# Attention with TensorE's order written out: eight transposes, logits of queries to come, value products of one step back

## The chip, the core and the metric

The kernel runs on one core of one Trainium2 chip. The metric is the device time of one execution in microseconds. The median of three runs of the kernel before is 3243.35 us (3238.03 to 3252.03).

## What is computed

One layer of a decoder trunk over 2048 tokens of 1024 channels in float32: a sparse attention mixer, then a SwiGLU feed-forward network, each followed by a LayerNorm. The change lies in the attention. Each query keeps its 256 best admissible keys (an indexer scores them), and 16 heads attend to the kept keys alone:

```python
_, sel = lax.top_k(score, topk)
valid = sel <= qp[None, :, None]
c_sel = jax.vmap(lambda cb, ib: cb[ib])(c_kv, sel)
logits = jnp.einsum('bqhc,bqkc->bhqk', ql, c_sel).astype(jnp.float32)
dist = (qp[None, :, None] - sel).astype(jnp.float32)
logits = logits - slopes[None, :, None, None] * dist[:, None]
logits = jnp.where(valid[:, None], logits, -jnp.inf)
p = jax.nn.softmax(logits, axis=-1).astype(c_sel.dtype)
return jnp.einsum('bhqk,bqkc->bqhc', p, c_sel)
```

## The kernel before, in words

The program has four stages in a row: projections and indexer scores; attention; the output projection; the feed-forward network. Nothing is gathered in attention. For each block of 128 queries a matrix S (SBUF, one row per query, one column per key up to the query's own block) ends up with the negative distance for a kept key and a very large negative number for every other key (the bit search of `topk_bits`, lines 412 to 454, then `select`, lines 490 to 504). All keys are then computed, and the others get probability zero.

`attention` (line 507) is called three times: for queries 0 to 1023, 1024 to 1535 and 1536 to 2047. Its unit is a group: 256 queries (two blocks, i = 0 and 1) for one pair of heads (e = 0 and 1), of which there are eight. The outer loop runs over pairs and, within a pair, over groups; in the second and third call the first group of some or all pairs is done ahead of the second (`EARLY`). A group does this:

- **Logits**, per head and block, and in the second and third call per half of the keys (a piece): GpSimd scales S by the head's slope into a tile `sm` (line 552, 14 buffers); TensorE multiplies queries `aqd` by keys `kka` or `kkb` into the PSUM tile `big` of two banks, two buffers (line 562, 128 output columns of the array); VectorE adds the two and reduces to the row's extreme `mx` (line 563); ScalarE takes the exponential in place with a row sum (line 567).
- **Transposes**: for each block of 128 keys (a key block) four 128x128 transposes of `sm`, two heads by two query blocks, go into one PSUM bank `tp` of three (line 585), and a copy moves it to `pt` (line 587, four buffers; on ScalarE in the first two calls, on ScalarE or VectorE as the scheduler chooses in the third).
- **Value products**: two products per key block, one for each head, accumulate into `oc` (line 589). Each has only 64 output columns (the head's width), head 0 in the lower and head 1 in the upper half of the partitions; each stands in the trace as two instructions. At the group's end VectorE copies `oc` out (line 592).

The source writes a group in one piece: all logits, then key block by key block transposes, copy, products. A list scheduler, which runs when the program is built and has its own model of time, takes the instructions by priority (about the order of the source) as their inputs become ready, and sets each engine's fixed order from that. So on TensorE logits of the next group stand among transposes and products of the current one wherever the scheduler put them. The DMA loads of keys (line 528), values (line 533) and queries (line 545) are issued from SyncE's queue.

The bit search for the last four query blocks and the selection for queries 1024 to 2047 run on ScalarE and VectorE at low priority beside the first call and the start of the second (a branch at line 479 is skipped when the search has settled everything).

Of the kernel before, what the change touches and what calls it, by code (L numbers as in the profile page):

```python
# [11 lines left out]
F32 = mybir.dt.float32  # L12
# [7 lines left out]
AF = mybir.ActivationFunctionType  # L20
# [5 lines left out]
P = 128  # L26
# [20 lines left out]
NSM, NAQ, NPT = 14, 2, 4  # L47
EARLY = 0, 5, 8
# [24 lines left out]
def trunk(tc, x, w_in, w_uk, w_uv, kv_g, w_o, w_gu, w_down, lm_g, lm_b, lf_g, lf_b, out, stop=99):  # L73
# [63 lines left out]
    def f(ap):  # L137
        return ap.bitcast(F32)
# [368 lines left out]
    def attention(ak, ap, apb, bk, qlo, nk, bnd, early, between={}):  # L507


        nw = 2 if nk > bnd else 1  # L510
# [5 lines left out]
        for at_, (j, groups) in enumerate(tasks):  # L516
            if at_ in between:
                between[at_]()
            mark["pair"] = tc.cur_priority
            kk, vv = [], []  # L520
            nkt = qlo + 256 * (groups[-1] + 1)
# [13 lines left out]
            for g in groups:  # L535
                q0 = qlo + g * 256
                b0 = q0 // P
                pr = {}
                total = sums_[:, g * 2:g * 2 + 2, 2 * j:2 * j + 2]
                su = ak.tile([P, 2, 2, 2], F32, name="su", tag="su", bufs=2) if nw == 2 else total.rearrange("p i (e w) -> p i e w", w=1)  # L540
                for e in range(2):
                    slope = float(np.float32(2.0 ** (-8.0 * (2 * j + e + 1) / H)))
                    qd = ak.tile([P, 2, 256], F32R, name="aqd", tag="aqd", bufs=NAQ)
                    for r in range(2):
                        nc.sync.dma_start(out=f(qd)[r * HD:(r + 1) * HD], in_=qs[j, :, e * HD:(e + 1) * HD, q0:q0 + 256].rearrange("c d t -> d c t"))
                    mx = ak.tile([P, 2, nw], F32, name="mx", tag="mx", bufs=4)
                    for i in range(2):
                        L = (b0 + i + 1) * P
                        pr[e, i] = []
                        for wi_, (w0, wn) in enumerate([(0, min(L, bnd)), (bnd, L - bnd)][:nw]):  # L550
                            sm = ap.tile([P, 1024], F32, name="sm", tag="sm", bufs=NSM)
                            nc.gpsimd.tensor_scalar(out=sm[:, :wn], in0=S[b0 + i][:, w0:w0 + wn], scalar1=slope, scalar2=1.0, op0=ALU.mult, op1=ALU.mult)  # L552
                            pr[e, i].append((w0, wn, sm))

# [5 lines left out]
                            for (s0, n) in [(0, first), (first, wn - first)][:1 + (wn > first)]:  # L560
                                for c in range(2):
                                    nc.tensor.matmul(o[:, s0:s0 + n], lhsT=qd[:, c, i * P:(i + 1) * P], rhs=kk[wi_][e][:, s0:s0 + n], start=(c == 0), stop=(c == 1))  # L562
                            nc.vector.tensor_tensor_reduce(out=sm[:, :wn], in0=o, in1=sm[:, :wn], scale=-1.0, scalar=mx[:, i, 0:1] if wi_ else 3.0e38,  # L563
                                                           op0=ALU.add, op1=ALU.min, accum_out=mx[:, i, wi_:wi_ + 1])
                    for i in range(2):
                        for wi_, (w0, wn, sm) in enumerate(pr[e, i]):
                            nc.scalar.activation(sm[:, :wn], sm[:, :wn], AF.Exp, bias=mx[:, i, nw - 1:nw], scale=-1.0, accum_out=su[:, i, e, wi_:wi_ + 1])  # L567
                if nw == 2:
                    nc.vector.tensor_reduce(out=total, in_=su, axis=AX.X, op=ALU.add)

                def prob(e, i, kb):
                    for (w0, wn, sm) in pr[e, i]:
                        if w0 <= kb * P < w0 + wn:
                            return sm[:, kb * P - w0:(kb + 1) * P - w0]
                pcopy = nc.scalar.copy if nk < T else nc.any.tensor_copy
                ob = bk("oc")

                for kb in range(b0 + 2):
                    i0 = 1 if kb == b0 + 1 else 0
                    n = (2 - i0) * P  # L580
                    tp = bk("tp")
                    for e in range(2):
                        for i in range(i0, 2):
                            at = e * n + (i - i0) * P
                            nc.tensor.transpose(tp[:, at:at + P], prob(e, i, kb), ident)  # L585
                    pt = ak.tile([P, 512], F32, name="pt", tag="pt", bufs=NPT)
                    pcopy(pt[:, :2 * n], tp[:, :2 * n])  # L587
                    for e in range(2):
                        nc.tensor.matmul(ob[e * HD:(e + 1) * HD, i0 * P:256], lhsT=vv[kb][:, e * HD:(e + 1) * HD],  # L589
                                         rhs=pt[:, e * n:(e + 1) * n], start=(kb == 0), stop=(kb == b0 + 1))  # L590
                ot = ak.tile([P, 256], F32, name="ot", tag="ot", bufs=2)
                nc.vector.tensor_copy(ot, ob[:, :256])  # L592
                store.dma_start(out=os_[j, :, q0:q0 + 256], in_=ot)
# [574 lines left out]
```

## Time and profile before

| | |
|---|---|
| median of 3 runs | 3243.35 us |
| the profiled execution | 3254.72 us, span 3252.9 us |
| TensorE busy, whole span | 3039.8 us (93%) |
| VectorE / ScalarE / GpSimd busy | 2024.7 / 1650.2 / 1557.6 us |
| attention in the span | from about 715 to about 1702 us |

The span runs from the first to the last instruction; 1.8 us of the execution lie around it. Busy times of the engines overlap one another. Windows are given in microseconds from the span's start. A busy TensorE is one with a matmul in flight, ends being modelled, so "busy throughout" doesn't say that the array works at its peak.

### The profile page before, as it was taken

To read this page: it belongs to the slowest core of one execution; us is meant where nothing else is said; L and a number is where in the kernel's file an instruction comes from. 1 tells how busy PE (TensorE), PEld (TensorE's weight loads), DVE (VectorE), ACT (ScalarE), POOL (GpSimd) and SP (SyncE) were. 2 spreads that over 40 slices of the span, in tenths; PEclk is the share of its full clock that TensorE was granted. 3 is DMA by queue.
4 is the path that set the end of the run, shared out by engine and by line. 5 is a ranking of instruction groups with operands and counts; after the bars stand their busy time and mean duration, and the time that the engine had idled before them with its cause. 6 is when DMAs were issued, how large, how long until landed. Compare 5 with 4: busy or idle time off the path is not lost.

```text
span 3252.9 us, 44786 instructions
## 1 busy us (share of the span) xinstructions
PE 3039.8 (93%) x15067; PEld 2283.1 (70%) x15067; DVE 2024.7 (62%) x3025; ACT 1650.2 (51%) x3169; POOL 1557.6 (48%) x1312
## 2 busy tenths in 40 slices
PE   7988889888888999999999989999989999999996
PEld 6777667665555666566667768888768888878875
DVE  3448798899468644444437675555675555336289
ACT  2536758549987777666662233333333333333333
POOL 3423324452234433433316456666776666645475
PEclk9999999989999999999999989999989999999998
DMA  9776556553344554866528643223233232655353
GB/s 293 241 237 196 185 170 187 181 155 106 104 130 128 161 148 118 195 167 171 150 85 252 209 152 110 100 101 104 98 127 109 101 111 92 216 162 175 110 165 134
DMA packets 460730, 499.00 MB, mean 153 GB/s; under 512 B 51408, under 2 KB 332112, under 8 KB 460496
## 3 DMA queue, kind: packets, MB, share of 16 engines
q1 hardware_dynamic: 369280, 359.09, 38.6%
q10 hardware_dynamic: 91216, 137.01, 11.8%
q8 instruction: 120, 1.97, 0.3%
q14 instruction: 114, 0.93, 0.1%
HBM read 359.01 MB, written 136.97 MB: 152 GB/s over the span
## 4 chain that ended last, share of the span: by engine, by line
PE 57%; DVE 7%; DMA 3%; issue 1%; POOL 0%; ACT 0%; SPq 0%; DVEq 0%; ACTq 0%; POOLq 0%
PE mm L221 8%; PE mm L219 8%; PE mm L220 8%; PE oc L589 7%; PE tp L585 7%; PE big L562 5%; PE mm L953 3%; PE mm L955 3%; PE mm L954 3%; PE mm L736 1%; PE mm L737 1%; PE mm L738 1%; DVE cl L144 1%; DVE hx L771 1%; PE tp L955 1%
## 5 line engine op out<-in xcount | busy, mean ns | idle before, releaser
L552 POOL TENSOR_SCALAR sm<-S 128x768 f32<-128x768 f32 (+7 forms) x384 | 330.8, 869 | 600.9 <-PE tp L585 564.2
L219 PE MATMUL mm<-ch,wh 128*128 128x512 f32 x1232 | 486.9, 396 | 16.1 <-ACT ch L766 14.9
L220 PE MATMUL mm<-cl,wh 128*128 128x512 f32 x1232 | 486.6, 395 | 8.0 <-DVE cl L144 5.9
L221 PE MATMUL mm<-ch,wl 128*128 128x512 f32 x1232 | 488.7, 397 | 0.0
L563 DVE CUSTOM_DVE_ANT_0 sm<-big,sm 128x1024 f32<-128x1024 f32 (+7 forms) x256 | 233.5, 922 | 242.2 <-POOL sm L552 125.0
L587 ACT COPY pt<-tp 128x512 f32<-128x512 f32 (+1 forms) x556 | 298.8, 558 | 151.8 <-PE tp L585 140.1
L567 ACT ACTIVATE sm<-sm,mx 128x768 f32<-128x768 f32 (+7 forms) x384 | 344.8, 901 | 56.6 <-DVE mx L563 55.6
L585 PEld LDWEIGHTS tp<-ident,sm 128*128 128x128 f32 x2176 | 234.8, 142 | 191.4 <-issue 181.1
L585 PE MATMUL tp<-ident,sm 128*128 128x128 f32 x2176 | 362.6, 289 | 2.7 <-ACT sm L567 1.8
L144 POOL TENSOR_TENSOR wl<-s,wh 128x512 fp32r<-128x512 f32 x176 | 239.5, 1366 | 192.4 <-ACT wh L819 192.4
L219 PEld LDWEIGHTS mm<-ch,wh 128*128 128x128 f32 x1232 | 234.4, 191 | 69.8 <-ACT ch L766 18.7
L220 PEld LDWEIGHTS mm<-cl,wh 128*128 128x128 f32 x1232 | 234.1, 190 | 66.5 <-DVE cl L144 10.2
L819 ACT CAST wh<-s 128x512 fp32r<-128x512 f32 x176 | 109.2, 621 | 331.3 <-PE mm L221 93.1
L562 PE MATMUL big<-kka,aqd 128*128 128x512 f32 (+3 forms) x896 | 234.9, 386 | 41.8 <-DVE mx L563 22.6
L221 PEld LDWEIGHTS mm<-ch,wl 128*128 128x128 f32 x1232 | 234.4, 190 | 50.4 <-POOL wl L144 0.2
L589 PE MATMUL oc<-pt,vva 128*64 128x256 f32 (+1 forms) x1536 | 237.3, 402 | 12.9 <-DVE ot L592 7.5
L144 POOL TENSOR_TENSOR wl<-wr,wh 128x512 fp32r<-128x512 f32 x132 | 190.9, 1447 | 94.7 <-ACT wh L819 91.5
L144 POOL TENSOR_TENSOR cl<-hx,ch 128x512 fp32r<-128x512 f32 (+2 forms) x106 | 153.2, 1448 | 153.1 <-ACT ch L948 133.1
L352 DVE SCALAR_TENSOR_TENSOR S<-rl,wi,S 128x768 f32<-128x768 f32 (+5 forms) x161 | 195.1, 1224 | 42.4 <-ACT rl L347 41.6
L562 PEld LDWEIGHTS big<-kka,aqd 128*128 128x128 f32 x896 | 157.5, 199 | 74.6 <-DVE mx L563 37.2
L948 ACT CAST ch<-hx 128x512 fp32r<-128x512 f32 (+2 forms) x158 | 94.7, 609 | 212.1 <-PE tp L954 93.8
L345 PE MATMUL big<-kst,qd 128*128 128x512 f32 (+2 forms) x624 | 163.5, 388 | 34.5 <-ACT rl L347 27.2
(293 smaller groups left out, 6703.5 us busy)
## 6 DMA issues: line engine op xcount, KB each, us to landing
wr<-in_f_w_gu SPq DMA_DIRECT2D x44, 1024.0 KB, 5.2
gs<-cc ACTq DMA_DIRECT2D x154, 256.0 KB, 2.0
hx<-gs SPq DMA_DIRECT2D x144, 256.0 KB, 2.9
aqd<-qs SPq DMA_DIRECT2D x256, 128.0 KB, 3.2
wraw<-in_a_w_in SPq DMA_DIRECT2D x56, 512.0 KB, 4.3
kka<-ks SPq DMA_DIRECT2D x96, 256.0 KB, 4.3
hx<-in_f_w_down SPq DMA_DIRECT2D x66, 256.0 KB, 3.0
qd<-qis SPq DMA_DIRECT2D x112, 128.0 KB, 4.6
```

Source lines behind the costliest of these rows:

```text
L144: (eng or nc.vector).tensor_tensor(out=lo, in0=src, in1=f(hi), op=ALU.subtract)
L219: nc.tensor.matmul(o, lhsT=lh, rhs=rh, start=(i == 0), stop=False)
L220: nc.tensor.matmul(o, lhsT=lh, rhs=rl, start=False, stop=False)
L221: nc.tensor.matmul(o, lhsT=ll, rhs=rh, start=False, stop=(i == n - 1))
L352: nc.vector.scalar_tensor_tensor(sv, rl[:, :wn], wi[:, h:h + 1], sv, op0=ALU.mult, op1=ALU.add)
L552: nc.gpsimd.tensor_scalar(out=sm[:, :wn], in0=S[b0 + i][:, w0:w0 + wn], scalar1=slope, scalar2=1.0, op0=ALU.mult, op1=ALU.mult)
L562: nc.tensor.matmul(o[:, s0:s0 + n], lhsT=qd[:, c, i * P:(i + 1) * P], rhs=kk[wi_][e][:, s0:s0 + n], start=(c == 0), stop=(c == 1))
L563: nc.vector.tensor_tensor_reduce(out=sm[:, :wn], in0=o, in1=sm[:, :wn], scale=-1.0, scalar=mx[:, i, 0:1] if wi_ else 3.0e38, op0=ALU.add, ...
L567: nc.scalar.activation(sm[:, :wn], sm[:, :wn], AF.Exp, bias=mx[:, i, nw - 1:nw], scale=-1.0, accum_out=su[:, i, e, wi_:wi_ + 1])
L585: nc.tensor.transpose(tp[:, at:at + P], prob(e, i, kb), ident)
L587: pcopy(pt[:, :2 * n], tp[:, :2 * n])
L589: nc.tensor.matmul(ob[e * HD:(e + 1) * HD, i0 * P:256], lhsT=vv[kb][:, e * HD:(e + 1) * HD], rhs=pt[:, e * n:(e + 1) * n], start=(kb == 0) ...
```

## The change

The three calls stay, and so do the kinds, numbers and sizes of the instructions. The loop over groups is rewritten. Two consecutive key blocks make a step: eight transposes (six in a group's last step), then up to two logits pieces of a later group (`PIECES`, at most one group ahead in the second and third call and two in the first, `AHEAD`, while fewer than 14 `sm` tiles are in use), then the four value products of the step before. From the first step of a call on, `tc.keep_in_program_order` holds TensorE to the order of the source; the other engines' orders are still the scheduler's.

```diff
+PIECES, AHEAD = {1: 2, 2: 2}, {1: 2, 2: 1}
...
+        def pe(ins):
+            if chained:
+                tc.keep_in_program_order(ins)
...
+            def turned(self, s):
+                out = []
+                for kb in (2 * s, 2 * s + 1):
...
+                            pe(nc.tensor.transpose(tp[:, at:at + P], self.prob(e, i, kb), ident))
...
+            def values(self, turned):
+                for kb, i0, n, pt in turned:
...
+                        pe(nc.tensor.matmul(self.ob[e * HD:(e + 1) * HD, i0 * P:256], lhsT=self.vv[kb][:, e * HD:(e + 1) * HD],
+                                            rhs=pt[:, e * n:(e + 1) * n], start=(kb == 0), stop=(kb == self.b0 + 1)))
...
+        for n, grp in enumerate(todo):
+            while not grp.ready:
+                piece()
+            for s in range(grp.steps):
+                now = grp.turned(s)
+                chained.append(1)
+                for _ in range(PIECES[nw]):
+                    if at_ < min(len(todo), n + 1 + AHEAD[nw]) and live[0] < NSM:
+                        piece()
+                behind()
+                behind = lambda grp=grp, now=now: grp.values(now)
+        behind()
```

How this moves TensorE's instructions, in the third call, inside the second groups of the pairs (16 key blocks each). L585 and L617 are the transposes, L562 and L589-with-`big` the logits, L589-with-`oc` and L628 the value products. Before:

```order
L562 MATMUL big<-kkb,aqd 128x512 x4
L562 MATMUL big<-kka,aqd 128x512 x4
L589 MATMUL oc<-pt,vvb 64x256 x2
L585 MATMUL tp<-ident,sm 128x128 x4
L589 MATMUL oc<-pt,vvb 64x128 x2
L585 MATMUL tp<-ident,sm 128x128 x8
L562 MATMUL big<-kkb,aqd 128x512 x2
L562 MATMUL big<-kkb,aqd 128x384 x2
L562 MATMUL big<-kka,aqd 128x512 x4
L589 MATMUL oc<-pt,vva 64x256 x2
L585 MATMUL tp<-ident,sm 128x128 x4
L589 MATMUL oc<-pt,vva 64x256 x2
```

And now:

```order
L617 MATMUL tp<-ident,sm 128x128 x8
L589 MATMUL big<-kka,aqd 128x512 x4
L589 MATMUL big<-kkb,aqd 128x512 x4
L628 MATMUL oc<-pt,vva 64x256 x4
L617 MATMUL tp<-ident,sm 128x128 x8
L628 MATMUL oc<-pt,vva 64x256 x4
L617 MATMUL tp<-ident,sm 128x128 x8
L628 MATMUL oc<-pt,vvb 64x256 x4
```

Products come in fours where they mostly came in twos. Counted over the three calls, unbroken runs of value products on TensorE were 510 and are 294 (of 1152 products). The last three or four steps of a group have no logits, since those of the next group are done by then.

On VectorE, around the branch at line 479 (480 now) that the selection of queries 1024 to 2047 waits for; "ISA sm" is the addition and reduction of one logits piece. Before:

```order
L592 COPY ot<-oc 128x256
L454 SCALAR_TENSOR_TENSOR hit,thr<-it_73,rank,m_6158 128x8
L473 TENSOR_REDUCE worst<-rank 128x1
L563 ISA sm,mx<-big,sm 128x1024
L563 ISA mx 128x1
```

And now:

```order
L455 SCALAR_TENSOR_TENSOR hit,thr<-it_73,rank,m_6158 128x8
L474 TENSOR_REDUCE worst<-rank 128x1
L590 ISA sm,mx<-big,sm 128x768
L590 ISA mx 128x1
L632 COPY ot<-oc 128x256
```

The rows ahead of the branch hold 113 such reductions before and 94 now, so the selection stands about five groups earlier in the work of attention. In the third call VectorE has 52 of the copies to `pt` now and had 20; ScalarE's share falls by the same 32.

## Rows read from the trace of the kernel before

**Rows 1.** Busy time by stretch: the first stretch holds top-k search and selection, the second neither.
```profile
core 0: us, PE busy (x) PEld busy (x) DVE busy (x) ACT busy (x) POOL busy (x), PEclk, DMA share, GB/s
715.00:1100.00 385.00, 330.85 (x1972) 206.48 (x1971) 290.04 (x527) 328.35 (x694) 143.54 (x169) 0.92 0.44 122
1100.00:1705.00 605.00, 597.05 (x3884) 373.71 (x3884) 265.13 (x529) 416.87 (x824) 202.69 (x226) 1.00 0.57 151
```

**Rows 2.** TensorE's waits, 1100 to 1705 (engine line <- releaser: us in total, times, longest).
```profile
PE oc L589 <- ACT pt L587: 4.2, 2, 2.3
PE big L562 <- DVE mx L563: 1.9, 1, 1.9
PE big L562 <- DMA aqd<-qs: 1.0, 1, 1.0
PE tp L585 <- ACT pt L587: 0.9, 1, 0.9
```

**Rows 3.** TensorE's timeline in the third call (start us, length us, engine line op, count).
```profile
1611.47 1.18 PE L562 MATMUL big<-kkb,aqd 128*128 128x512 f32 x4
...
1613.50 0.65 PE L589 MATMUL oc<-pt,vvb 128*64 128x256 f32 x4
...
1615.04 1.09 PE L585 MATMUL tp<-ident,sm 128*128 128x128 f32 x8
1615.88 1.05 PE L562 MATMUL big<-kkb,aqd 128*128 128x512 f32 x4
...
1618.38 0.66 PE L585 MATMUL tp<-ident,sm 128*128 128x128 f32 x4
1618.96 0.65 PE L589 MATMUL oc<-pt,vva 128*64 128x256 f32 x4
1619.55 0.66 PE L585 MATMUL tp<-ident,sm 128*128 128x128 f32 x4
1620.13 1.08 PE L589 MATMUL oc<-pt,vva 128*64 128x256 f32 x8
1621.15 0.66 PE L585 MATMUL tp<-ident,sm 128*128 128x128 f32 x4
1621.56 1.18 PE L562 MATMUL big<-kkb,aqd 128*128 128x512 f32 x4
...
1636.63 1.18 PE L562 MATMUL big<-kkb,aqd 128*128 128x512 f32 x4
```

**Rows 4.** Waits of weight loads, 715 to 1100.
```profile
PEld tp L585 <- issue: 56.6, 154, 0.8
```

**Rows 5.** TensorE's timeline: first and last runs of value products of each stretch.
```profile
733.85 1.12 PE L589 MATMUL oc<-pt,vva 128*64 128x256 f32 x4
...
1098.72 0.44 PE L589 MATMUL oc<-pt,vvb 128*64 128x128 f32 x4
...
1100.84 0.65 PE L589 MATMUL oc<-pt,vva 128*64 128x256 f32 x4
...
1700.98 1.30 PE L589 MATMUL oc<-pt,vvb 128*64 128x256 f32 x12
```

**Rows 6.** Value products alone, by stretch.
```profile
715.00:1100.00 385.00, 118.39 (x760) 41.77 (x760) 0.92 0.44 122
1100.00:1705.00 605.00, 237.46 (x1544) 80.12 (x1544) 1.00 0.57 151
```

**Rows 7.** TensorE's waits, 715 to 1100.
```profile
PE big L562 <- DVE mx L563: 25.3, 26, 3.2
PE big L562 <- DMA aqd<-qs: 15.7, 9, 4.4
PE oc L589 <- DVE ot L592: 7.5, 5, 4.5
```

**Rows 8.** Costliest groups of the page: scaling, exponential, copy to `pt`.
```profile
L552 POOL TENSOR_SCALAR sm<-S 128x768 f32<-128x768 f32 (+7 forms) x384 | 330.8, 869 | 600.9 <-PE tp L585 564.2
...
L567 ACT ACTIVATE sm<-sm,mx 128x768 f32<-128x768 f32 (+7 forms) x384 | 344.8, 901 | 56.6 <-DVE mx L563 55.6
L587 ACT COPY pt<-tp 128x512 f32<-128x512 f32 (+1 forms) x556 | 298.8, 558 | 151.8 <-PE tp L585 140.1
```

**Rows 9.** Groups by line: the read of the exponential's row sum, whole span.
```profile
L567 ACT ACTIVATION_READ_ACCUMULATOR sm<-sm,mx 128x1 f32 x384 | 74.8, 195 | 0.0
```

**Rows 10.** Groups by line, VectorE, 1100 to 1705.
```profile
L563 DVE CUSTOM_DVE_ANT_0 sm<-big,sm 128x1024 f32<-128x1024 f32 (+1 forms) x110 | 122.3, 1112 | 172.1 <-POOL sm L552 101.1 <-PE big L562 68.5 <-POOL hx L682 1.6
L563 DVE CUSTOM_DVE_ANT_0 sm<-big,sm,mx 128x768 f32<-128x768 f32 (+2 forms) x111 | 110.1, 992 | 106.7 <-PE big L562 85.7 <-POOL sm L552 15.1 <-DVE mx L563 2.1
L563 DVE DVE_READ_ACCUMULATOR2_ANT mx<- 128x1 f32 x221 | 18.4, 83 | 0.0
L587 DVE COPY pt<-tp 128x512 f32<-128x512 f32 x20 | 13.8, 689 | 6.2 <-PE tp L585 5.8
```

**Rows 11.** DMA issues of the page: queries (KB each, us to landing).
```profile
aqd<-qs SPq DMA_DIRECT2D x256, 128.0 KB, 3.2
```

**Rows 12.** VectorE's timeline: a scan of the selection.
```profile
1000.86 3.70 DVE L501 TENSOR_TENSOR_SCAN ft<-one,sr,u 128x1280 f32<-128x1280 f32 x1
```

More of the change, by code (lines that the diff above doesn't have):

```diff
@@ L515, in attention, with task @@
         tasks = [(j, first) for j in range(early)] + [(j, second) for j in range(early)] + [(j, range(ng)) for j in range(early, NPAIR)]
-        for at_, (j, groups) in enumerate(tasks):
-            if at_ in between:
-                between[at_]()
+        work = [(i, j, g, g == groups[0], qlo + 256 * (groups[-1] + 1)) for i, (j, groups) in enumerate(tasks) for g in groups]
+        keys, live, chained = {}, [0], []
+        pcopy = nc.scalar.copy if nk < T else nc.any.tensor_copy
+        def pe(ins):
+            if chained:
+                tc.keep_in_program_order(ins)
+        def task(i, j, nkt):
+            if i in between:
+                between[i]()
             mark["pair"] = tc.cur_priority
             kk, vv = [], []
-            nkt = qlo + 256 * (groups[-1] + 1)
             for i, (k0, k1) in enumerate([(0, min(bnd, nkt)), (bnd, nkt)][:nw]):
@@ L534, in attention, with __init__, logits @@
                 vv += [v[:, k] for k in range((k1 - k0) // P)]
[L535 to L538, printed above, removed]
+            return kk, vv
+        class Group:
+            def __init__(self, i, j, g, new, nkt):
+                self.i, self.j, self.g, self.new, self.nkt = i, j, g, new, nkt
+                self.q0 = qlo + g * 256
+                self.b0 = self.q0 // P
+                self.steps = (self.b0 + 2) // 2
+                self.pr = {}
+                self.gen = self.logits()
+                self.ready = False
+            def logits(self):
+                j, g, b0, pr = self.j, self.g, self.b0, self.pr
+                if self.new:
+                    keys[self.i] = task(self.i, j, self.nkt)
+                kk, self.vv = keys[self.i]
                 total = sums_[:, g * 2:g * 2 + 2, 2 * j:2 * j + 2]
@@ L564, in attention @@
                                                            op0=ALU.add, op1=ALU.min, accum_out=mx[:, i, wi_:wi_ + 1])
[L565 to L579, printed above, removed]
+                            if (i, wi_) == (1, nw - 1):
+                                for i_ in range(2):
+                                    for w_, (_, n, sm) in enumerate(pr[e, i_]):
+                                        nc.scalar.activation(sm[:, :n], sm[:, :n], AF.Exp, bias=mx[:, i_, nw - 1:nw], scale=-1.0, accum_out=su[:, i_, e, w_:w_ + 1])
+                                if nw == 2 and e == 1:
+                                    nc.vector.tensor_reduce(out=total, in_=su, axis=AX.X, op=ALU.add)
```

34 lines of the change are left out of this document (26 added, 8 removed).

## The prediction

> **What bounds the kernel now.** I read the busy times by stretch first, because attention is two regimes [rows 1]. From 1100 to 1705 us TensorE is busy 597 of 605 us at a granted clock of 1.00 (the 2.4 GHz level), ScalarE 417, VectorE 265 and GpSimd 203. Nothing but TensorE can set the pace there, and its list of waits adds up to 8 us [rows 2]. From 715 to 1100 us no engine is full: TensorE is busy 331 of 385 us at 0.92, ScalarE 328, VectorE 290, because the top-k search and the selection share ScalarE and VectorE with attention. So I expect the change to act through TensorE's own time in the second stretch, and weakly in the first.
>
> The second view is TensorE's timeline, for what "busy" hides [rows 3]. The instructions don't cost the same in every neighbourhood. A run of value products with four instructions (one key block) takes 0.59 us from its first start to the next instruction (1618.96 to 1619.55), a run of eight 1.02 us (1620.13 to 1621.15). So the second key block costs 0.43, and each run carries 0.15 to 0.16 us that doesn't depend on its length. The transposes ahead of products carry as much: four transposes before products take 0.58 (1618.38 to 1618.96), while four more transposes before logits cost only 0.84 - 0.41 = 0.43 us (1615.04 to 1615.88 with eight, 1621.15 to 1621.56 with four). That is another 0.15. The trace shows the two together as **0.30 us for every separate run of value products**: about half is paid going in and half coming out, where the matmuls change from 128 output columns to 64 and back (128*128 and 128*64 in the rows). The weight loads show it too: those of transposes sit idle with no releaser, 0.37 us on average, 154 times in the first stretch [rows 4]. Between transposes and logits, both of 128 columns, I see no such cost.
>
> **The change part by part.** *The runs of products.* The timeline has 165 runs between 715 and 1100 and 345 between 1100 and 1705 (the first and last of each in [rows 5]), 510 in all, and the order now has 294. The products there are 760 and 1544 instructions [rows 6]; a step of the new order makes one run of eight, so 760 / 8 = 95 and 1544 / 8 = 193, and with the few runs still broken near the calls' first groups 98 and 196.
>
> Second stretch: 345 - 196 = 149 runs at 0.30 us = **45 us less**, all on the engine that sets the end. One group tests it: the 25.16 us from 1611.47 to 1636.63 hold 15 runs, and the new order gives such a group 8, so 7 x 0.30 = 2.1 us less, 23.1 us.
>
> Here a rule says less. The Trainium skill (TensorEngine Tiling (Array Packing), Key Properties) states that a change of the tiling mode drains TensorE, which agrees in kind with [rows 3]. Its page TensorE: Matmul & The Clock Gate (Part 2) gives a pipeline drain as some 128 cycles; two drains at 2.4 GHz are an estimated 0.11 us, and by that figure the 149 runs would give 16 us instead of 45. The measurement is 0.30, and I go by it.
>
> First stretch: 165 - 98 = 67 runs, 20 us of TensorE's time. How much of it counts, the trace doesn't show, since TensorE idles 54 of 385 us there. At the least it is nothing or a loss (ScalarE is busy 85% of the stretch and none of its work goes away); at the most it is the 20 us and about half of the 48 us of waits in [rows 7], since the selection now stands five groups earlier and products read copies that are a whole step old: 45 us. The rows nearest to it are ScalarE's 328 and TensorE's 331 us, level with each other, so I take a good third of the 20 us, **8 us less**.
>
> *What takes over behind TensorE.* In the second stretch a step with logits now takes, from [rows 3]: eight transposes 0.58 + 0.43 = 1.01, two pieces of logits 2.0 in the third call (1611.47 to 1613.50) and by their columns, 1216 for 1792, some 1.4 in the second, products 1.02, together 3.4 to 4.0 us. ScalarE has two copies and two exponentials with their sum reads in it, 2 x 0.558 + 2 x (0.901 + 0.195) = 3.3 us [rows 8, 9], and in the third call VectorE takes some of the copies. VectorE has two reductions, 1.11 + 0.99 + 2 x 0.08 = 2.3, plus at times a copy of 0.69 [rows 10]. GpSimd has two scalings of 0.87 [rows 8] in the same order as before. A step without logits takes 2.0 us against two copies, 1.1 us, so ScalarE catches up there. The products' copies have a whole step to arrive. It fits, closely in the second call.
>
> *The fixed order.* A logits piece that finds its PSUM buffer not yet reduced now holds up the products and transposes behind it on TensorE, and through them the copies, the exponentials and the next `sm` tiles. Between a piece's end and the next use of its buffer lie products 1.02, transposes 1.01 and one other piece of 0.5 us or more: at least 2.5 us against 2.3 us of reductions. The trace before has no such order; its nearest row is the 1.9 us that logits waited for VectorE in the second stretch [rows 2]. Below, nothing is lost and the 8 us of waits may shrink; above, each of the 32 groups of the second and third call could wait once for a whole copy, 32 x 0.56 = 18 us. I take **5 us more**, as [rows 2] lie nearer to nothing.
>
> *Edits at nothing.* The loads keep their number. A load of queries takes 3.2 us [rows 11] and needs its buffer free; that happens two logits steps ahead of the next use, over 6 us, so it stays hidden. More copies on VectorE (32 x 0.69 = 22 us) lie in its idle half; without that cover they would delay the reductions. Output projection and feed-forward are untouched and only start earlier.
>
> Sum: -45 - 8 + 5 = **-48 us**. Against its own execution (3254.7 us, 11.4 above the median) that is 3206.7; against the median of 3243.35, 3195. I give the second.
>
> **The rivals.** *The first stretch gains fully.* If the earlier selection removes the waits of [rows 7] as far as bounded above, 45 + 45 = 90 us less, 3153. For it speaks that VectorE was the late one (25.3 us, 26 times), against it ScalarE at 85%.
>
> *ScalarE becomes the bound.* It is busy 69% of the second stretch, 417 of 605; squeezed into 560 it would be some 400 of 560 after the copies that move away. If its queue, in order, puts exponentials that wait for reductions ahead of copies, the steps run at its pace: the 18 us above and the first stretch's gain gone, 3243 - 45 + 18 = 3216; with twice that wait 3234. The Trainium skill (Perfetto Trace Analysis, Identifying the Most-Contended Engine) holds matmul busy time to be a poor measure and asks for the weight loads' busy share instead: 374 of 605 is 62%, below ScalarE's 69%, so by that page ScalarE is the one to look at and little would be gained. Against it: TensorE was hardly ever released by another engine there [rows 2].
>
> *Slower: logits at the head of the line.* In the first stretch VectorE executes scans of 3.7 us between reductions [rows 12]. Before, the scheduler had put transposes and products where it expected such holes; now everything stands behind the logits. Of 384 pieces [rows 8] 221 lie behind 1100 us [rows 10], so 163 pieces or 82 steps with logits lie here. If each waited 1 us more, 82 us are lost against 53 gained: 3243 + 29 = 3272. It decides from 53 / 82 = 0.65 us a step on. Against it: logits waited for VectorE 26 times before, 1 us each, and the one-step delay of the products leaves ScalarE more room.
>
> *Nothing changes.* If the scheduler's order had been the same in effect, 3243; the count of 294 runs for 510 rules this out nearly.
>
> **How the numbers follow.** Forecast 62%; full first stretch 16%; ScalarE as the bound 15%; slower 5%; nothing 2%. The range takes in the forecast with its terms' bounds, the first rival and the ScalarE rival to 3226. It leaves out the slow case, no change, a third of the ScalarE rival and what lies below 3153, some 17%. A measurement of this kernel can tell about 0.5%, 16 us, from no change: under 3227 is faster, over 3260 slower. The ScalarE rival ends above 3227 in about a third of its cases: so faster 0.62 + 0.16 + 0.10 = 0.88, same 0.07, slower 0.05.
>
> **What would show it.** In the new profile the second stretch should be some 565 us long, with runs of eight products at 1.02 us, transposes in eights, and groups of the last kind every 23.1 us. Right for the wrong reason: if the time falls but the interval from a run's first product to the next transpose isn't about 1.02 us. Wrong: if TensorE's waits for VectorE or ScalarE in the second stretch grow from 8 us to over 30, or if TensorE idles over 80 us in the first.

## The result, and the profile after

The changed kernel takes 3204.16 us (median of four runs, 3196.54 to 3209.03), the kernel before 3247.69 (median of four, with one more run than the three shown ahead). The ratio is 0.9854, 95% interval 0.9833 to 0.9874, and the difference of the medians is 43.5 us. The profiled executions differ by a little more, 3252.9 - 3199.8 = 53.1 us of span, since that of before lies 7.0 above its median and that of after 2.6 below.

| | before | after |
|---|---|---|
| the profiled execution | 3254.72 us | 3201.61 us |
| attention's last value product starts | 1701.9 us | 1646.2 us |
| separate runs of value products | 510 | 294 |
| TensorE busy, whole span | 3039.8 us (93%) | 2964.9 us (93%) |

All of it is won by the end of attention: its last product starts 55.7 us earlier (its first transpose already 1.7), and the rest of the program gives 2.6 us back. To compare stretches with the same work in them I cut at the 760th product instruction, where the prediction's two stretches met: at 1098.9 us before, at 1082.3 after. Busy times of both kernels by these stretches, of before first:

```profile
core 0: us, PE busy (x) PEld busy (x) DVE busy (x) ACT busy (x) POOL busy (x), PEclk, DMA share, GB/s
715.00:1099.00 384.00, 329.85 (x1966) 205.62 (x1964) 289.04 (x525) 327.35 (x692) 143.54 (x169) 0.92 0.44 123
1099.00:1702.00 603.00, 595.05 (x3879) 372.23 (x3877) 264.06 (x527) 416.03 (x822) 202.69 (x226) 1.00 0.58 151
```

And after:

```profile
715.00:1082.00 367.00, 302.75 (x1951) 207.41 (x1951) 285.29 (x519) 324.70 (x693) 168.86 (x169) 0.93 0.43 127
1082.00:1647.00 565.00, 555.58 (x3891) 391.48 (x3888) 290.07 (x565) 393.42 (x788) 202.87 (x226) 0.99 0.64 162
```

In the second stretch TensorE's busy time fell by 39.5 us, with nearly the same number of instructions, and the stretch by 38: TensorE idled 8 us before and 9 after. In the first stretch TensorE's busy time fell by 27 us, but it idles 64 us where it idled 54, so only 17 came out.

TensorE's timeline of the third call after the change (start us, length us, engine line op, count) answers to [rows 3]:

```profile
1567.32 1.08 PE L628 MATMUL oc<-pt,vva 128*64 128x256 f32 x8
...
1590.36 1.08 PE L628 MATMUL oc<-pt,vva 128*64 128x256 f32 x8
...
1619.04 1.17 PE L589 MATMUL big<-kka,aqd 128*128 128x512 f32 x4
1620.05 1.08 PE L589 MATMUL big<-kkb,aqd 128*128 128x512 f32 x4
1621.06 1.08 PE L628 MATMUL oc<-pt,vva 128*64 128x256 f32 x8
1622.08 1.09 PE L617 MATMUL tp<-ident,sm 128*128 128x128 f32 x8
1623.10 1.08 PE L628 MATMUL oc<-pt,vva 128*64 128x256 f32 x8
1624.11 1.09 PE L617 MATMUL tp<-ident,sm 128*128 128x128 f32 x8
```

From a run's first product to the next transpose it is 1.02 us (1621.06 to 1622.08), from a step's transposes to its products again 1.02, and two groups of the last kind begin 23.04 us apart (1567.32, 1590.36) where it was 25.16.

TensorE's waits after the change, in the first stretch (715 to 1082), which answer to [rows 7]:

```profile
PE big L589 <- DVE mx L590: 21.8, 18, 3.2
PE tp L617 <- ACT pt L619: 21.2, 17, 2.5
PE tp L617 <- ACT sm L595: 8.6, 8, 2.4
PE tp L617 <- DMA vva<-vs: 4.5, 1, 4.5
PE oc L628 <- DVE ot L632: 3.7, 3, 2.1
PE oc L628 <- ACT pt L619: 3.1, 4, 1.8
PE big L589 <- DMA aqd<-qs: 0.2, 1, 0.2
```

And in the second (1082 to 1647), which answer to [rows 2]:

```profile
PE oc L628 <- ACT pt L619: 3.7, 5, 2.9
PE tp L617 <- ACT sm L595: 3.1, 2, 2.9
PE tp L617 <- ACT pt L619: 1.8, 1, 1.8
PE tp L617 <- DVE u L663: 0.7, 1, 0.7
```

The waits for the queries' load, 15.7 us, are gone from the first stretch. In their place transposes wait for ScalarE's copies and exponentials, 30 us together. From 1310 us to the end of attention TensorE waits for nothing at all.

### The profile page after: what moved, and what is told of

Read it like the earlier page. It is cut to its first block, busy times and chain, and to the rows that moved or that the text cites. A ratio compares the mean times of both kernels' runs of the same rounds, so it can differ in the third digit from the quotient of the medians.

```text
span 3199.8 us, 44751 instructions
## 1 busy us (share of the span) xinstructions
PE 2964.9 (93%) x15067; PEld 2297.5 (72%) x15067; DVE 2049.9 (64%) x3057; ACT 1622.7 (51%) x3137; POOL 1588.1 (50%) x1312
## 4 chain that ended last, share of the span: by engine, by line
PE 58%; DVE 7%; DMA 3%; issue 1%; ACT 1%; POOL 1%; SPq 0%; DVEq 0%; ACTq 0%; POOLq 0%
PE mm L221 8%; PE mm L222 8%; PE mm L220 8%; PE tp L617 7%; PE oc L628 7%; PE big L589 6%; PE mm L1016 2%; PE mm L1014 2%; PE mm L1015 2%; DVE cl L145 1%; PE mm L797 1%; PE mm L798 1%; PE mm L799 1%; DVE hx L832 1%; PE tp L1015 1%
## 5 line engine op out<-in xcount | busy, mean ns | idle before, releaser
L578 POOL TENSOR_SCALAR sm<-S 128x768 f32<-128x768 f32 (+7 forms) x384 | 356.3, 936 | 517.7 <-PE tp L617 459.2
L619 ACT COPY pt<-tp 128x512 f32<-128x512 f32 (+1 forms) x524 | 278.8, 566 | 166.1 <-PE tp L617 166.1
L617 PE MATMUL tp<-ident,sm 128*128 128x128 f32 x2176 | 316.8, 285 | 40.3 <-ACT pt L619 23.0
L617 PEld LDWEIGHTS tp<-ident,sm 128*128 128x128 f32 x2176 | 237.2, 143 | 149.9 <-issue 98.2
L589 PE MATMUL big<-kka,aqd 128*128 128x512 f32 (+3 forms) x896 | 233.7, 387 | 22.0 <-DVE mx L590 21.6
L628 PE MATMUL oc<-pt,vva 128*64 128x256 f32 (+1 forms) x1536 | 207.2, 388 | 7.4 <-DVE ot L632 3.7
L348 ACT ACTIVATE rl<-big 128x768 f32<-128x768 f32 (+5 forms) x184 | 143.0, 790 | 101.5 <-PE big L346 47.2
```

The lines of the kernel that those rows point to most:

```text
L589: pe(nc.tensor.matmul(o[:, s0:s0 + n], lhsT=qd[:, c, i * P:(i + 1) * P], rhs=kk[wi_][e][:, s0:s0 + n], start=(c == 0), stop=(c == 1)))
L617: pe(nc.tensor.transpose(tp[:, at:at + P], self.prob(e, i, kb), ident))
L628: pe(nc.tensor.matmul(self.ob[e * HD:(e + 1) * HD, i0 * P:256], lhsT=self.vv[kb][:, e * HD:(e + 1) * HD], rhs=pt[:, e * n:(e + 1) * n], st ...
```

## Experiments

"The change" is the changed kernel, 3204 us with 294 runs of products. Ratios are against the kernel before, run on the same chip beside each. Its median there was 3247.7 us for the change; 3250.5 for one block per step, the same in the first call alone, products in the same step and two steps per run; 3256.6 for one block with products two back, the scheduler's order, two steps in the second call and shared copies; 3249.7 for the other four. So medians of different sets can differ by up to 9 us for that reason alone, and the ratios are the safer comparison. The last columns are read from the profiled execution of each kernel: when the last product of the first call starts, and how long the second and third call take from there to the last product of all.

| kernel | runs of products | median us | ratio, 95% interval | first call's end | calls 2 and 3 |
|---|---|---|---|---|---|
| before | 510 | 3247.69 | | 1039.7 | 662.2 |
| the change | 294 | 3204.16 | 0.9854 (0.9833 to 0.9874) | 1030.6 | 615.6 |
| one block per step | 574 | 3335.65 | 1.0271 (1.0243 to 1.0300) | 1086.0 | 697.6 |
| one block, first call alone | 371 | 3245.79 | 0.9985 (0.9970 to 1.0000) | 1083.4 | 609.0 |
| products in the same step | 291 | 3312.83 | 1.0201 (1.0176 to 1.0225) | 1068.9 | 689.3 |
| one block, products two back | 574 | 3282.61 | 1.0086 (1.0060 to 1.0113) | 1067.9 | 662.6 |
| the same, first call alone | 371 | 3226.46 | 0.9929 (0.9901 to 0.9956) | 1059.6 | 604.2 |
| order left to the scheduler | 376 | 3231.67 | 0.9924 (0.9899 to 0.9949) | 1048.7 | 631.5 |
| two steps per run | 167 | 3211.07 | 0.9873 (0.9851 to 0.9894) | 1049.9 | 607.3 |
| the same, second call alone | 255 | 3203.45 | 0.9840 (0.9798 to 0.9881) | 1046.2 | 604.3 |
| copies shared in all calls | 294 | 3207.77 | 0.9846 (0.9804 to 0.9888) | 1044.6 | 602.7 |
| both of these | 254 | 3198.69 | 0.9836 (0.9801 to 0.9870) | 1049.2 | 606.1 |
| 128 columns | 291 | 3331.02 | 1.0247 (1.0210 to 1.0283) | 1053.2 | 716.1 |
| 128 columns, one block | 574 | 3359.36 | 1.0338 (1.0298 to 1.0378) | 1086.3 | 714.3 |

My theory was that the number of runs is what the change bought, 0.30 us each. The rival was that the fixed order and the delay of the products by a step did it.

### One block per step

```diff
-PIECES, AHEAD = {1: 2, 2: 2}, {1: 2, 2: 1}
+PIECES, AHEAD = {1: 1, 2: 1}, {1: 2, 2: 1}
...
-                self.steps = (self.b0 + 2) // 2
+                self.steps = self.b0 + 2
...
-                for kb in (2 * s, 2 * s + 1):
+                for kb in (s,):
```

> The changed kernel with steps of one key block: four transposes, one piece of logits, then the products of the step before. Order fixed and products one step back as in the change, but 574 separate runs of value products where the change has 294 and the kernel before 510. Theory (each separate run costs TensorE 0.30 us, and the number of runs is what the change bought): 280 more runs, 280 x 0.30 = 84 us over the changed kernel's 3204, so about 3288, slower than the kernel before by some 40; the stretch of the second and third call, with 196 runs in the change and 414 here, is longer by 65 us, and the first call by some 5 to 23. Rival (the gain comes from the fixed order and the delay of the products by a step, the runs cost nothing): within 15 us of 3204. A third reading (a run costs the 0.11 us of an estimated drain): 3235.

Measured: 3336, 131 us above the change, where 280 runs should have cost 84. The excess shows in TensorE's waits over all of attention (715 to 1784); the products now wait for their own copies, 57 us against 7 in the change:

```profile
PE oc L628 <- ACT pt L619: 56.7, 52, 2.2
PE oc L628 <- DVE ot L632: 30.8, 20, 4.2
```

So the edit mixed two things. "One step back" is only one block back here, and a copy has half the time to arrive. It neither confirms nor refutes 0.30.

### One block, first call alone

The same edit where `qlo` is 0.

> The changed kernel with steps of one key block in the first call of attention alone: 371 runs of products, 77 more than the change, all in the first call. It tests how much of TensorE's time in the first stretch counts. The prediction took a good third: 77 x 0.30 = 23 us of TensorE's time, of which 8 to 9 end up in the total, so about 3213. If TensorE sets the pace there too: 3227. If ScalarE and VectorE alone set it: 3204.

Measured: 3246, outside all three: 42 us for 77 runs. It has the same fault as the run before: 27 us of waits of products for copies (22 times) in its first call.

### Products in the same step

```diff
-                behind()
-                behind = lambda grp=grp, now=now: grp.values(now)
-        behind()
+                grp.values(now)
```

> The changed kernel with the products in the same step, behind the logits of that step and not one step back; 291 runs of products, as many as in the change. The two copies have only two pieces of logits (1.4 to 2.0 us) to arrive, where they need 2 x 0.56 us after the transposes. Theory (the number of runs is what counts): little in the second and third call, where steps have logits between, +5 to +15 us for the steps without logits, whose products then follow the transposes directly and wait for the copies (some 0.6 us each); total 3210 to 3225. Rival (the delay by one step is what bought the time): the whole gain goes, about 3248 or above.

Measured: 3313. The theory was wrong here by 90 us, and the rival right: without the step of delay the whole gain goes, and 65 us more. TensorE's waits in attention (715 to 1765) and its timeline in the third call account for it:

```profile
PE oc L628 <- ACT pt L619: 126.0, 163, 5.8
```
```profile
1603.40 1.09 PE L617 MATMUL tp<-ident,sm 128*128 128x128 f32 x8
1604.78 1.14 PE L628 MATMUL oc<-pt,vvb 128*64 128x256 f32 x8 [0.29 <-ACT pt L619]
1605.86 1.09 PE L617 MATMUL tp<-ident,sm 128*128 128x128 f32 x8
1607.52 1.14 PE L628 MATMUL oc<-pt,vvb 128*64 128x256 f32 x8 [0.57 <-ACT pt L619]
```

The waits rose from 7 to 126 us, the total by 109, at the same number of runs. In a fixed order long runs are worth nothing unless their operands have had time to come. I then went on with two causes, runs and lateness, and separated them.

### One block, products two back

On top of the first experiment's edit:

```diff
-        behind = lambda: None
+        behind = [lambda: None] * 2
...
-                behind()
-                behind = lambda grp=grp, now=now: grp.values(now)
-        behind()
+                behind.pop(0)()
+                behind.append(lambda grp=grp, now=now: grp.values(now))
+        behind.pop(0)()
+        behind.pop(0)()
```

> One key block per step as in the first experiment, but the products two of these steps back, so that a copy has as long to arrive as in the change (about two blocks' transposes and logits); 574 runs of products. It takes the lack of delay away and leaves the number of runs. Theory now (two causes: 0.30 us per separate run, and copies that arrive too late when products come sooner than a step of two blocks): no waits of products for ScalarE's copies; the second and third call, 615.6 us in the change, take 615.6 + 203 x 0.30 = 677 us (they took 697.6 with one block back), the first call 308 + 77 x 0.30 = 331 (362 with one block back); total 3204 + 84 = 3288. Rival (the number of runs costs nothing, the 131 us of the first experiment were all lateness): about 3204. Rival (a run costs more than 0.30, and lateness nothing): near 3336 again.

Measured: 3283, 5 us under the theory's figure, far from either rival. The waits of products for copies are 13 us, so the difference to the first experiment, 53 us between the medians and 60 by the ratios, comes with the delay alone. Busy time by call, of the change (from 1031) and of this kernel (from 1068):

```profile
1031.00:1310.00 279.00, 265.07 (x1846) 186.79 (x1846) 135.31 (x303) 204.77 (x446) 113.37 (x140) 0.98 0.65 166
1310.00:1647.00 337.00, 337.00 (x2358) 237.70 (x2355) 182.80 (x326) 225.37 (x427) 110.36 (x114) 1.00 0.63 159
```
```profile
1068.00:1351.00 283.00, 280.67 (x1843) 175.71 (x1841) 127.97 (x294) 204.42 (x437) 108.39 (x136) 1.00 0.60 157
1351.00:1731.00 380.00, 374.95 (x2353) 219.38 (x2351) 148.83 (x274) 255.04 (x481) 111.27 (x115) 0.99 0.56 145
```

TensorE is busy 655.6 us in the second and third call against 602.1, with the same instructions: 53.5 us for 203 more runs, 0.26 each. But the agreement of the totals is partly made of something else: the calls took 662.6 us where the theory gave 677, and the first call 340 where it gave 331.

### 128 columns, with two blocks and with one

```diff
-                        pe(nc.tensor.matmul(self.ob[e * HD:(e + 1) * HD, i0 * P:256], lhsT=self.vv[kb][:, e * HD:(e + 1) * HD],
-                                            rhs=pt[:, e * n:(e + 1) * n], start=(kb == 0), stop=(kb == self.b0 + 1)))
+                        pe(nc.tensor.matmul(self.ob[:, i0 * P:256], lhsT=self.vv[kb],
+                                            rhs=pt[:, e * n:(e + 1) * n], start=(kb == 0 and e == 0), stop=(kb == self.b0 + 1 and e == 1)))
```

The second kernel of the pair has this and the edits of "one block, products two back".

> The changed kernel with value products of 128 output columns: the values of both heads are the weights of every product, and both heads' products are added into one tile (this changes the output: each half holds the sum over both heads with the wrong head's values in it). 291 runs of eight, order and delay as in the change. It has no meaning by itself but beside the next run. If the two heads' products, which write different halves of a tile, ran side by side until now, each key block takes up to 0.43 us more on TensorE, 576 x 0.43 = 248 us, so between 3204 and 3450. Theory (the price of a run is the change of output columns from 128 to 64 and back): no surcharge at either end of a run; four transposes cost 0.43 us before products as before logits.

> The same 128-column products, both heads added into one tile, with steps of one key block and the products two steps back: 574 runs instead of 291, the pair of the kernel with 574 runs of 64 columns (3283, against 3204 for 294). Theory (a run costs because the columns change): within 15 us of the run before this one. Rival (each change from one kind of instruction to another costs, whatever the columns, or the pipeline empties at each): 283 x 0.28 = 79 us above the run before this one.

Measured: 3331 and 3359, 28 us apart, between the two expectations. The busy times by call tell why. Two blocks, then one:

```profile
1053.00:1363.00 310.00, 303.98 (x1839) 273.31 (x1838) 130.13 (x295) 204.37 (x442) 109.07 (x136) 0.99 0.59 149
1363.00:1770.00 407.00, 405.90 (x2370) 359.31 (x2369) 161.86 (x294) 239.62 (x458) 110.05 (x114) 1.00 0.52 132
```
```profile
1086.00:1395.00 309.00, 304.83 (x1837) 269.34 (x1836) 128.65 (x293) 206.83 (x438) 108.61 (x136) 0.99 0.56 149
1395.00:1801.00 406.00, 404.13 (x2360) 352.12 (x2359) 164.16 (x295) 246.86 (x458) 109.96 (x114) 1.00 0.50 132
```

In the second and third call, where TensorE sets the pace, 204 more runs cost nothing: 709.0 us of TensorE's time against 709.9. All of the difference, 33 us, arose in the first call. TensorE's timelines in the third call, two blocks and one, show the same in the small:

```profile
1660.04 1.04 PE L617 MATMUL tp<-ident,sm 128*128 128x128 f32 x8
1660.92 1.89 PE L628 MATMUL oc<-pt,vvb 128*128 128x256 f32 x8
1662.65 0.82 PE L617 MATMUL tp<-ident,sm 128*128 128x128 f32 x6
```
```profile
1690.07 0.60 PE L617 MATMUL tp<-ident,sm 128*128 128x128 f32 x4
1690.50 1.03 PE L628 MATMUL oc<-pt,vvb 128*128 128x256 f32 x4
1691.37 0.60 PE L617 MATMUL tp<-ident,sm 128*128 128x128 f32 x4
```

Eight transposes take 0.88 us, four 0.43; eight products 1.73, four 0.87. There is no part that doesn't depend on the length. The weight loads of the transposes agree. Their waits with no releaser (us in total, times, longest), the sign that [rows 4] gave, come about once per run of products in attention of the change (715 to 1647) and of "one block, products two back" (715 to 1731), and are all but gone in the pair (715 to 1770 and 1801):

```profile
PEld tp L617 <- issue: 98.2, 285, 0.8
PEld tp L617 <- issue: 212.8, 568, 0.8
```
```profile
PEld tp L617 <- issue: 0.6, 3, 0.2
PEld tp L617 <- issue: 2.4, 12, 0.2
```

So what a run costs comes with the change between 128 and 64 output columns, and it is gone when the columns stay. With 128 columns the two heads' products no longer run side by side either, so the pair doesn't tell the change of width from the beginning and end of running side by side. The Trainium skill (TensorEngine Tiling (Array Packing), Key Properties) has it so in kind, that a changed tiling mode drains TensorE. The 0.11 us per run that the prediction estimated from the drain figure of the Trainium skill's page TensorE: Matmul & The Clock Gate (Part 2) is less than half of what the runs show.

### The same delay, first call alone

The edits of "one block, products two back" where `qlo` is 0.

> Steps of one key block with the products two such steps back, in the first call alone; 77 runs more than the change, with the same delay for the copies. With one block back this edit cost 42 us in total. If that was the 77 runs, on TensorE's path entirely and dearer than 0.30 us, 3240 or more again. Theory (runs and lateness are two costs): 77 x 0.30 = 23 us of TensorE's time, all of which counts if TensorE sets the pace of the first call (3227), a third of which by the prediction's weighting (3212), none if ScalarE and VectorE set it (3204). In the kernel with one block everywhere the first call was 37 us longer than in the change, part of which later calls gave back, so I expect 3220 to 3230.

Measured: 3226, the figure for "all of it counts". I don't take it for a proof. Busy times of the first call, in the change and here:

```profile
723.00:1031.00 308.00, 252.18 (x1621) 171.38 (x1622) 249.25 (x445) 284.82 (x604) 142.60 (x135) 0.93 0.40 117
```
```profile
720.00:1060.00 340.00, 279.99 (x1632) 168.10 (x1633) 258.13 (x453) 292.06 (x610) 126.31 (x138) 0.90 0.37 108
```

TensorE is busy 28 us longer and idle 4 us longer, which speaks for the runs (77 x 0.27 = 21). But the 128-column pair has the same lengthening of the first call, 33 us, by an edit under which runs cost nothing elsewhere; there it is 15 us of busy time, at a granted clock of 0.90 for 0.94, and 18 us of waiting (two blocks, then one):

```profile
720.00:1053.00 333.00, 286.61 (x1616) 247.17 (x1617) 256.91 (x451) 288.25 (x608) 127.25 (x138) 0.94 0.38 108
720.00:1086.00 366.00, 301.83 (x1627) 255.10 (x1628) 259.45 (x453) 294.20 (x610) 127.97 (x138) 0.90 0.35 100
```

With one-block steps the products also wait for `oc` to be copied out, 30 us in this kernel for 4 in the change. The granted clock helps to divide the busy time. Between the levels of 1.2 and 2.4 GHz, a mean of 0.93 over 308 us is some 43 us at the lower one, and 0.90 over 340 us some 68; for the pair it is 40 and 73. Work takes nearly twice as long there (see the last section), so I estimate that about half of the added time, 12 us here and 16 in the pair, is the clock. That leaves some 16 of the 28 us for the 77 runs, 0.2 each, and nothing of the pair's 15 for its runs. So the runs are about half of the lengthening here, by this estimate; no run shows it alone.

### Order left to the scheduler

```diff
-            if chained:
-                tc.keep_in_program_order(ins)
+            pass
```

> The changed kernel with the order of TensorE's instructions left to the scheduler: the same source (pieces of logits, two-block steps, products a step back), nothing held in program order; 376 runs of products where the change has 294. By the runs alone 82 x 0.30 = 25 us more: 3229. If what the fixed order brings is the delay of the products, which the scheduler gives up where it expects an operand to be ready, there are waits of products for copies besides, and it comes near the kernel before: 3240 to 3250. If the rewritten source and its early logits are the gain, and not the fixed order: 3204.

Measured: 3232, what the number of runs says (3229), with nothing on top for lateness: the products wait for copies 2 us in all of attention, so the scheduler's order leaves the copies time too. In the second and third call TensorE is busy 619.6 us for 602.1, with 61 more runs, 0.29 each. About half of the change's gain, 0.8% of 1.5%, is thus had by the rewritten source alone, and the fixed order adds the rest: its 82 fewer runs at 0.27 us are 22 us of the 23 that the ratios give. In the first call (723 to 1049) the waits for queries are back, which the fixed order had removed:

```profile
PE big L588 <- DMA aqd<-qs: 17.1, 14, 3.9
```

### Two steps per run, in all calls and in the second alone

```diff
-NSM, NAQ, NPT = 14, 2, 4
+NSM, NAQ, NPT = 13, 2, 6
...
+        def flush():
+            for g_, t_ in waiting:
+                g_.values(t_)
+            waiting.clear()
...
-                behind()
-                behind = lambda grp=grp, now=now: grp.values(now)
-        behind()
+                if len(waiting) == 2 or (waiting and waiting[0][0] is not grp):
+                    flush()
+                waiting.append((grp, now))
+        flush()
```

In the second kernel the 2 is `2 if qlo == 1024 else 1`.

> The changed kernel with the products of two steps issued together, so runs of 16 (six buffers for the copies in place of four, 13 for the logits in place of 14): 167 runs where the change has 294. Theory: 127 fewer runs x 0.30 = 38 us less if all of it counts; 80 of the 127 lie in the second and third call, so 24 us there for sure and 5 to 14 in the first: 3166 to 3175. Rival (the price of a run is no longer on the path, or buffers now run out and stall the transposes): 3200 or above.

> Products of two steps in one run in the second call alone (with six buffers for copies and 13 for logits in all calls): 255 runs, 52 in place of 92 in the second call. In the kernel with two steps everywhere the second call took 265.9 us where the change takes 279.2, and 40 x 0.30 = 12 us was the theory's figure; the first call lost 19 and the third 5 us by waits of transposes for copies. Theory (those losses come from the two-step runs and not from the buffers): second call 266, the others as in the change, total 3192. Rival (one buffer less for the logits is what lost): the first call is longer again and the total 3204 or above.

Measured: 3211 and 3203, no gain over the change that the intervals show. The first has the rival's figure; the second's interval (some 3182 to 3209 us by the ratios) holds the theory's 3192 as well as the rival's 3204, so the total doesn't decide there. TensorE's time does fall: with two steps everywhere and 95 fewer runs, the second and third call keep it busy 583 us for 602, 0.20 each. It is lost again in two places. TensorE's waits in the third call (1316 to 1657) and around the start of attention (690 to 745), both of two steps everywhere:

```profile
PE tp L617 <- ACT pt L619: 14.4, 15, 1.1
```
```profile
PE big L589 <- DMA aqd<-qs: 13.6, 2, 12.6
```

Steps without logits now issue sixteen transposes in a row into three `tp` banks and wait for copies; and attention's first transpose starts at 733 instead of 723 us. That second loss comes with the buffers, not with the runs: the kernel with two steps in the second call alone, whose first call issues as the change does, has it too (733.7), and its first call ends 16 us later than in the change. SyncE's queue shows where it begins. With two steps everywhere the first loads of keys (line 538) wait for a product of the projections (690 to 745):

```profile
SPq L538 <- PE mm L222: 25.7, 1, 25.7
```

They are issued from 718 us on, in the change before 703. The other two kernels with these buffers have the same wait, 25.8 and 25.7 us, and the change doesn't have it. It fits keys' tiles that lie, with these buffers, in memory that the projections still use; no run shows that, and the buffers weren't changed alone.

### Copies shared in all calls, alone and together with two-step runs in the second call

```diff
-        pcopy = nc.scalar.copy if nk < T else nc.any.tensor_copy
+        pcopy = nc.any.tensor_copy
```

> The copies of transposed probabilities are shared between ScalarE and VectorE in all three calls (the scheduler chooses; 105 on VectorE where the change has 52, all in the third call). It tests what holds the first call after the change: there transposes wait for ScalarE's copies and exponentials (27 us before 1010 us) and logits for VectorE's reductions (22 us). If ScalarE is the bound of the first call: it gets some 10 to 20 us shorter, total 3185 to 3195. If VectorE with its searches and scans is: the copies delay reductions, logits wait more, and it is 5 to 20 us slower.

> A candidate: two-step runs in the second call (254 runs of products) and copies shared between ScalarE and VectorE in all calls. Alone, the first gave 3203 and the second 3208, where the change has 3204. Theory (TensorE sets the pace of the second call and 40 runs fewer are worth 0.30 us each once copies are not late): 3190. Rival (what these edits gain in the second call is only time that the first lost, since the first call's end is late by as much): 3200 to 3210.

Measured: 3208 and 3199. In the first call of the former (715 to 1045) transposes wait less for ScalarE's copies, 14.1 us for 21.2, and logits more for VectorE, 29.5 us for 18.2 (723 to 1031 in the change):

```profile
PE big L589 <- DVE mx L590: 29.5, 19, 4.9
PE tp L617 <- ACT pt L619: 14.1, 14, 2.3
```

So neither engine alone holds the first call. It ends 14 us later than in the change (and begins 4 later), yet the second call's last product starts at 1307 for 1310 us, and the total is the same: what the first call loses the second gives back, as the expectation for the combined kernel said of its rival. In the second call TensorE idles 4.6 us for 13.9 there, and is busy 257.4 us for 265.1 at a granted clock of 1.00 for 0.98, with as many runs. The combined kernel has the lowest median of all. It lies between the theory's 3190 and the rival's 3200, and its interval holds both and lies across that of the change, so I can't call it faster.

## Why the prediction was right

**TensorE's own time in the second stretch.** Forecast: 149 runs fewer, 45 us. Measured: 39.5 us of busy time, 0.265 per run. Eleven of the kernels above have 64-column products; for ten, all but the one with products in the same step, and for the kernel before, the busy time of TensorE in the second and third call stands against the number of runs there:

| runs | 116 | 170 | 171 | 211 (four kernels) | 272 | 370 (before) | 414 (two kernels) |
|---|---|---|---|---|---|---|---|
| TensorE busy, us | 583 | 595 | 593 | 597, 598, 601, 602 | 620 | 645 | 656, 662 |

A straight line through them has 0.27 us per run and misses none by over 6 us. The kernel left out was busy 615 us with 208 runs, 13 above the line; its products wait for copies 163 times in attention, and no run shows whether the 13 us come from that. That the term hangs on 64 columns among 128 is shown by the 128-column pair; its size, 0.30 read from four places of one timeline, was a tenth too large.

**The fixed order.** Forecast 5 us of new waits in the second stretch; the waits there are 9 us now and the idle time was 8, and none of them is a logits piece that waits for VectorE. The head-of-line loss didn't come in that stretch. What a fixed order costs when operands are late shows on the products instead, in the kernel without the delay: 126 us of waits. The prediction gave the delay one sentence ("The products' copies have a whole step to arrive."); the experiments give it as much weight as the runs.

**The first stretch.** Forecast 8 us, from 20 us of TensorE's time, a good third of which counts. Up to the same product it was 17 us, twice that: TensorE's busy time fell by 27 and its idle time rose by 10. Of the 27, 67 runs at 0.27 us are 18. The granted clock of 0.93 for 0.92 is some 51 us at the lower level for 61, an estimated 5 us more, a term that the prediction didn't have; the last 4 stay open. Counted to the first call's last product it was 9. So this term was mis-sized, though its bounds (nothing to 45) held. The part of the rival that expected the waits of [rows 7] to vanish was half right: those for queries went (15.7 to 0.2), those for `mx` stayed (25.3 to 21.8), and ScalarE's copies and exponentials came instead, 30 us. So the ScalarE rival took place, in part, in the first stretch and not in the second, where TensorE waits for it 9 us. The Trainium skill's advice (Perfetto Trace Analysis, Identifying the Most-Contended Engine) to judge by the weight loads' share, one of its two measures, would have pointed to ScalarE in the second stretch; the shares of weight loads and ScalarE are now 69% and 70%, and ScalarE still holds TensorE up for no more than those 9 of 565 us.

**The sum.** 48 forecast; 55.7 in attention and 53.1 in the span of the profiled executions, 43.5 between the medians, so 3204 us where 3195 was forecast. In the profiled executions the second stretch gave 38 us for 40 (45 less 5): the smaller price per run and the waits that didn't come nearly made up for each other. The first gave 17 for 8, and nothing made up for that. That the medians lie nearer to the forecast than these 55 us is chance: the profiled execution of before was 7 us above its median. Of the forecast's tests, the second stretch is 565 us long as said, runs of eight take 1.02 us, groups come every 23.04 us for 23.1, and TensorE idles 64 us in the first stretch, under the 80 that would have spoken against it.

## What to carry to other kernels

Read what an instruction costs beside its neighbours, not only what it costs: matmuls of 64 output columns among matmuls of 128 pay 0.27 us per separate run here, and grouping them is free time for the engine that sets the end. A fixed order earns that only when each operand gets a step of other work to arrive; without it the same order lost 109 us. Where three engines are nearly level, as in the first call, a gain on one comes back as a wait for another, so judge an edit by the end of the whole and not of one call.

## What the runs showed of the hardware beyond that

- The two heads' products, which write different halves of a PSUM tile with 64 columns each, run side by side: in the trace their instructions start in pairs, 7 ns apart, with 0.22 to 0.27 us from one pair to the next (third call of the change), where with 128 columns they start one by one, 0.22 us apart. A further key block costs 0.43 us (four trace instructions), and 0.87 with 128 columns. In the third call this explains the longer time: 406.5 - 336.4 = 70 us, and 119 runs x 0.27 = 32 us saved, are 102 us for 240 key blocks, 0.43 each.
- In the first call the granted clock lay between the levels of 1.2 and 2.4 GHz: 0.93 with TensorE idle 56 of 308 us (the change), 0.94 with 46 of 333 and 0.90 with 64 of 366 (128 columns, two blocks and one), 0.90 with 60 of 340 and 0.87 with 71 of 360 (one block in the first call alone, products two back and one back). More idle time mostly went with a lower clock, but not in step: 18% idle stands beside both 0.93 and 0.90. Where the clock was 0.50 (728 to 738 us in the change), five transposes ahead of logits took 0.98 us; at 1.00 eight took 0.84 [rows 3]. Time at the lower level lengthens the busy time: the last of these kernels has TensorE busy 289 us where the one before it needs 280 for the same number of runs.
